# Hymba layer on one Trainium2 core: the seven-product up-projection in more chunks of both half-steps

## Chip, core and metric

The kernel runs on one core of one Trainium2 chip. The metric is the device time of one execution in microseconds (us). Before the change it is 1837.93 us, the median of three runs (1836.93 to 1838.51).

In the profile the engines are PE (TensorE, matmuls), PEld (its weight loads), DVE (VectorE), ACT (ScalarE), POOL (GpSimd) and SP (which issues the DMAs). L127 is line 127 of the kernel before.

## The reference, cut to what matters

One layer of a decoder, batch 1, 256 tokens, width 2048, everything in float32. A half-step is a gated feed-forward with inner width 5632; there are two of them, around a mixer of attention and a state-space part (S5).

```python
def rmsnorm(x, g):
    xf = x.astype(jnp.float32)
    y = xf * lax.rsqrt(jnp.mean(xf * xf, axis=-1, keepdims=True) + EPS)
    return (y * g.astype(jnp.float32)).astype(x.dtype)

def swiglu(x, w1, w3, w2):
    return (jax.nn.silu(x @ w1) * (x @ w3)) @ w2
...
        h = h + 0.5 * swiglu(rmsnorm(h, ffn1_norm[l]), ffn1_w1[l], ffn1_w3[l], ffn1_w2[l])
        proj = rmsnorm(h, mix_norm[l]) @ w_in[l]
...
        a = nsa_mixer(q, kc, vc, ksl, vsl, kw, vw, gates, rel_bias,
...
        s = s5_mixer(u_ssm, ssm_lam_re[l], ssm_lam_im[l], ssm_log_step[l], ssm_b_re[l], ssm_b_im[l],
...
        h = h + jnp.concatenate([a, s], axis=-1) @ w_out[l]
        h = h + 0.5 * swiglu(rmsnorm(h, ffn2_norm[l]), ffn2_w1[l], ffn2_w3[l], ffn2_w2[l])
    return rmsnorm(h, final_norm)
```

## The kernel before

**A product of float32.** PE multiplies float32r. Each operand is therefore split in a high part, a rounded copy made by ScalarE (L127), and a low part, the remainder, made by VectorE (L128), which needs the high part. A product is three matmuls: high x high, high x low, low x high. The activations are split once (`xh`, `xl`); the weights are split as they come: a DMA brings 256 rows x 512 columns (512 KB) into a tile `raw` (five buffers), and a pair of splits of 128x1024 makes `whi` and `wlo` (three buffers each). One such tile feeds 12 matmuls of 512 columns. Tiles called `wk` come from a pool of 48.

**A half-step** (`ffn`) goes through the inner width in 11 chunks of 512 columns. A chunk c has an up part (x @ w1 and x @ w3 over 16 blocks of the width, that is 8 pairs of blocks), the gates, 16 small transposes of the gates (L414) whose result is split again, and a down part (@ w2), which is done one chunk later: the order on PE is up(c), down(c-1) columns 0 and 1, transposes(c), down(c-1) columns 2 and 3. The results are added to `h` by VectorE (L357).

**Seven products.** In the second half-step the up part of every chunk runs through `up_wino`. For some pairs of blocks (`WINO`: 1, 3, 5) the 2x2 block product (two blocks of tokens x two blocks of the width, times w1 and w3 of two blocks) is done with seven block products in place of eight, after Winograd: 21 matmuls in place of 24. The price is sums. Of the weights: four sums of 128x512 (L318) and their splits, on VectorE and ScalarE, for each pair in each chunk; only w1 is split as a whole, of w3 one half. Of the activations ("left factor"): four sums per pair, made once, in `combine`, from the transposed activations while the output projection ends. The products are gathered in PSUM: `mm` (four banks: products 1, 5, 6, 7), `tp` (two banks: product 2 with the plain pairs' w1, product 3 with their w3, for the first tokens) and `sd` (two banks, the other tokens). `up_wino` thus uses all eight banks; the transposes use `tp` too. After the last pair of `WINO` VectorE gathers products 1, 5, 6 and 7 in four instructions (L336 to L339). Pairs not in `WINO` are "plain". In the first half-step all chunks are plain (L180 to L182).

**Side work.** Generators in `sides` get one step at each plain weight tile (`tick`). In the first half-step that is the preparation of S5 (`prepare`): it waits 40 tiles, then does a step at every second tile. A step is what stands between two `yield` in `s5_prepare`: 5 steps, then 28 for powers, 4 for products with B, 20 for matrices (with transposes and small matmuls on PE and copies out of PSUM, L598 and L612), and 24 for eight tables (L627, L628, L630), 81 in all. `up_wino` gives no step; the down parts of all chunks do.

**What sets the order.** A scheduler places all instructions on the engines' queues by priority as its own model of time sees them fit; each engine then runs its queue in that order, PE included. The splits of weights have a higher priority (`offset=50`). A buffer is taken when its former content has been read, so an instruction that fills a buffer waits for the readers.

Of the kernel before, what the change touches and what calls it, by code (L numbers as in the profile page):

```python
# [21 lines left out]
F32 = mybir.dt.float32  # L22
F32R = mybir.dt.float32r
# [18 lines left out]
WMAX = 536  # L42
WINO = (1, 3, 5)
WROW = 1152
# [27 lines left out]
def hymba_layer(tc, x, ffn1_norm, ffn1_w1, ffn1_w3, ffn1_w2, mix_norm, w_in,  # L72
# [22 lines left out]
    def work(shape, dtype=F32):  # L95
        return sp.tile(shape, dtype, name="wk", tag="wk")
# [106 lines left out]
    class Norm:  # L203
# [10 lines left out]

        def combine(self, pair, ps, scales):

            y, s = work([128, 2, T]), work([128, 4, 128])
            for k in range(2):
                S.activation(y[:, k, :], ps[:, k, :], AF.Identity, scale=scales[k])
            a11, a21, a12, a22 = (y[:, k, t * 128:t * 128 + 128] for k in range(2) for t in range(NT))  # L220
            V.tensor_tensor(s[:, 0, :], a21, a22, ALU.subtract)
            V.tensor_tensor(s[:, 2, :], a11, a21, ALU.subtract)
            V.tensor_tensor(s[:, 1, :], s[:, 0, :], a11, ALU.subtract)
            V.tensor_tensor(s[:, 3, :], a12, s[:, 1, :], ALU.add)
            sh, sl = work([128, 4, 128], F32R), work([128, 4, 128], F32R)
            split(sh, sl, s)
            self.wino[pair] = sh, sl

        def cols(self, n, wino=()):
            xh = xp.tile([128, 4, T], F32R, name="xh", tag="xh")  # L230
            xl = xp.tile([128, 4, T], F32R, name="xl", tag="xl")
            for kp in range(2):
                ps = tp_tile().rearrange("p (k t) -> p k t", k=2)
                for k in range(2):
                    kt = 4 * n + 2 * kp + k
                    for tt in range(NT):
                        PE.transpose(ps[:, k, tt * 128:tt * 128 + 128], h[:, tt, kt * 128:kt * 128 + 128], ident)
                for k in range(2):
                    g = self.gain * 16 + 4 * n + 2 * kp + k
                    split(xh[:, 2 * kp + k, :], xl[:, 2 * kp + k, :], ps[:, k, :], par[:, g:g + 1])  # L240
                if 2 * n + kp in wino:
                    g = self.gain * 16 + 4 * n + 2 * kp
                    self.combine(2 * n + kp, ps, [par[:, g + k:g + k + 1] for k in range(2)])
            self.x.append((xh, xl))
            self.square(n)
# [23 lines left out]

    def ffn(w1, w3, w2, xs, rstd, done, by_tokens=False, wino=()):  # L270
        last = FF // 512 - 1

        def up_wino(c):
# [25 lines left out]
            for p in range(KT // 2):  # L299
                raw1, raw3 = (wload(w[p * 256:p * 256 + 256, f], 512)[:, :, :512] for w in (w1, w3))  # L300
                end = p == KT // 2 - 1
                if p not in wino:
                    with tc.high_priority(offset=50):
# [5 lines left out]
                    continue  # L309
                done_ = p == max(wino)  # L310
                with tc.high_priority(offset=50):
# [77 lines left out]

        prev = None  # L390
        for c in range(FF // 512 + 1):
            if c < FF // 512 and wino:
                gates = up_wino(c)
# [275 lines left out]
    def prepare():  # L669
        for _ in range(40):  # L670
            yield
        for _ in s5_prepare():
            yield
            yield
        bias_prepare()
# [12 lines left out]
    prep = prepare()  # L688
    sides.append(prep)
    ffn(ffn1_w1[0], ffn1_w3[0], ffn1_w2[0], n1, n1.rstd(), nm.cols)  # L690
    drain(prep)
# [329 lines left out]
    for k0 in (8, 0):  # L1021
        if k0 == 0:
            drain(attn)
        for n in range(4):
# [4 lines left out]
            if k0 == 0:  # L1029
                n2.cols(n, WINO)  # L1030
    nf = Norm(0)
# [38 lines left out]

    ffn(ffn2_w1[0], ffn2_w3[0], ffn2_w2[0], n2, n2.rstd(), finish, by_tokens=True, wino=WINO)
    ctx.close()
# [23 lines left out]
```

## Time and profile before

| | us |
|---|---|
| median of 3 runs | 1837.93 |
| the profiled execution | 1839.61 |
| its span, first to last instruction | 1837.7 |
| PE busy | 1808.9 (98%) |
| PE weight loads | 1509.9 (82%) |
| VectorE busy | 1391.5 (76%) |
| ScalarE busy | 895.9 (49%) |

How to read it: matmuls overlap in the profile. A row's duration runs from its start to a modelled end, and the next one starts before that. How fast PE goes through its work is seen from start to start. The first half-step reaches to about 760 us, the second begins at about 1115 us; chunks take 64 to 70 us.

### The profile page before, as it was taken

The page shows a single profiled execution, that of the slowest core. Times are in us where ns is not written, and L with a number is a line of the kernel's source. Part 1 is how long each engine was busy: PE and PEld are TensorE (multiplying, and loading weights), DVE is VectorE, ACT ScalarE, POOL GpSimd, SP SyncE. Part 2 cuts the span into 40 slices and gives each one's busy share as a digit, 9 for nine tenths or more (in the row PEclk, how much of TensorE's full clock was granted, in tenths as well). Part 3 has the DMA queues.
Part 4 walks back from the last instruction along what each step waited for, and adds up shares of the span by engine and source line. Part 5 has one row for each costly group of instructions (what it writes and reads, how often), then busy time and mean ns, then how long its engine had stood idle before and what let it go on. Part 6 is the DMA issues. An engine that isn't in the chain of part 4 may idle for free. (4 is left out here: it accounts for less than half of the span.)

```text
span 1837.7 us, 24559 instructions
## 1 busy us (share of the span) xinstructions
PE 1808.9 (98%) x9266; PEld 1509.9 (82%) x9266; DVE 1391.5 (76%) x2003; ACT 895.9 (49%) x1233; POOL 14.7 (1%) x32
## 2 busy tenths in 40 slices
PE   8999999999999999999999999999999999999997
PEld 6888888888888888899988787788888888888886
DVE  5477666787987465789885668878887888789786
ACT  6434444433444444555537656545554554455454
POOL 0000000000000000000000000000000000000002
PEclk9999999999999999999999999999999999999999
DMA  7676666655566665555574366556666666666563
GB/s 240 188 214 188 193 186 193 185 174 180 179 194 190 194 191 188 171 152 152 147 220 143 111 187 187 194 182 199 192 206 185 204 206 194 194 195 204 179 205 135
DMA packets 193290, 340.88 MB, mean 185 GB/s; under 512 B 21034, under 2 KB 30868, under 8 KB 193172
## 3 DMA queue, kind: packets, MB, share of 16 engines
q1 hardware_dynamic: 193172, 339.31, 60.3%
q8 instruction: 73, 1.20, 0.3%
q14 instruction: 45, 0.37, 0.1%
HBM read 337.16 MB, written 2.11 MB: 185 GB/s over the span
## 5 line engine op out<-in xcount | busy, mean ns | idle before, releaser
L127 ACT ACTIVATE whi<-raw 128x1024 fp32r<-128x1024 f32 (+1 forms) x587 | 620.7, 1060 | 769.5 <-PE mm L182 499.9
L128 DVE SCALAR_TENSOR_TENSOR wlo<-raw,whi 128x1024 fp32r<-128x1024 f32 (+1 forms) x587 | 716.7, 1223 | 342.6 <-ACT whi L127 338.8
L180 PE MATMUL mm<-whi,xh 128*128 128x512 f32 x832 | 327.6, 394 | 2.0 <-ACT whi L127 2.0
L181 PE MATMUL mm<-wlo,xh 128*128 128x512 f32 x832 | 326.2, 392 | 0.0
L182 PE MATMUL mm<-whi,xl 128*128 128x512 f32 x832 | 325.7, 392 | 0.0
L180 PE MATMUL mm<-whi,wk 128*128 128x512 f32 x688 | 270.1, 393 | 0.0
L182 PE MATMUL mm<-whi,wk 128*128 128x512 f32 x688 | 268.2, 390 | 0.0
L181 PE MATMUL mm<-wlo,wk 128*128 128x512 f32 x688 | 268.0, 390 | 0.0
L180 PEld LDWEIGHTS mm<-whi,xh 128*128 128x128 f32 x832 | 156.6, 188 | 34.7 <-ACT whi L127 2.4
L181 PEld LDWEIGHTS mm<-wlo,xh 128*128 128x128 f32 x832 | 156.7, 188 | 33.0 <-DVE wlo L128 1.1
L182 PEld LDWEIGHTS mm<-whi,xl 128*128 128x128 f32 x832 | 156.6, 188 | 32.0 <-DVE xl L128 0.4
L182 PEld LDWEIGHTS mm<-whi,wk 128*128 128x128 f32 x688 | 129.1, 188 | 26.8
L180 PEld LDWEIGHTS mm<-whi,wk 128*128 128x128 f32 x688 | 129.2, 188 | 26.6 <-issue 0.6
L181 PEld LDWEIGHTS mm<-wlo,wk 128*128 128x128 f32 x688 | 129.3, 188 | 25.9
L357 DVE SCALAR_TENSOR_TENSOR h<-mm,h 128x512 f32<-128x512 f32 x176 | 114.3, 683 | 3.2 <-PE mm L369 2.5
L191 PE MATMUL mm<-xh,whi 128*128 128x256 f32 x384 | 112.7, 294 | 0.9 <-DVE wk L983 0.9
L127 ACT ACTIVATE wk<-wk 128x512 fp32r<-128x512 f32 x139 | 83.5, 626 | 55.5 <-DVE wk L318 49.7
L192 PE MATMUL mm<-xh,wlo 128*128 128x256 f32 x384 | 108.8, 283 | 0.0
L193 PE MATMUL mm<-xl,whi 128*128 128x256 f32 x384 | 108.8, 283 | 0.0
L284 PE MATMUL tp<-whi,xh 128*128 128x512 f32 x253 | 98.7, 391 | 2.2 <-DVE wk L128 1.1
L286 PE MATMUL tp<-wlo,xh 128*128 128x512 f32 x253 | 98.9, 392 | 1.2 <-DVE wlo L128 1.2
L287 PE MATMUL tp<-whi,xl 128*128 128x512 f32 x253 | 98.4, 390 | 0.0
(301 smaller groups left out, 2409.8 us busy)
## 6 DMA issues: line engine op xcount, KB each, us to landing
raw<-in_ffn_w_dram SPq DMA_DIRECT2D x528, 512.0 KB, 3.9
raw<-in_w_in_dram SPq DMA_DIRECT2D x48, 512.0 KB, 3.7
raw<-in_w_out_dram SPq DMA_DIRECT2D x32, 512.0 KB, 3.7
raw<-in_w_in_dram SPq DMA_DIRECT2D x8, 536.0 KB, 4.2
raw<-in_glu_w_dram SPq DMA_DIRECT2D x8, 512.0 KB, 4.6
h<-in_x_dram SPq DMA_DIRECT2D x4, 512.0 KB, 8.4
raw<-in_cmp_w_k_dram SPq DMA_DIRECT2D x4, 512.0 KB, 4.6
raw<-in_cmp_w_v_dram SPq DMA_DIRECT2D x4, 512.0 KB, 6.9
```

What stands on the lines that cost most here:

```text
L127: S.activation(hi, src, AF.Copy if isinstance(scale, float) else AF.Identity, scale=scale)
L128: V.scalar_tensor_tensor(lo, src, scale, hi.bitcast(F32), op0=ALU.mult, op1=ALU.subtract)
L180: PE.matmul(o, xh[:, t], hi[:, i, :n], start=kt == k0, stop=False)
L181: PE.matmul(o, xh[:, t], lo[:, i, :n], start=False, stop=False)
L182: PE.matmul(o, xl[:, t], hi[:, i, :n], start=False, stop=kt == k1 - 1)
L191: PE.matmul(o, wh, xh, start=kt == 0 and q % 2 == 0, stop=False, skip_group_check=True)
L192: PE.matmul(o, wl, xh, start=False, stop=False, skip_group_check=True)
L193: PE.matmul(o, wh, xl, start=False, stop=last, skip_group_check=True)
L284: PE.matmul(o, xh, wh, start=id(o) not in begun, stop=False)
L286: PE.matmul(o, xh, wl, start=False, stop=False)
L287: PE.matmul(o, xl, wh, start=False, stop=stop)
L357: V.scalar_tensor_tensor(o, p, 0.5, o, op0=ALU.mult, op1=ALU.add)
```

## The change

`WINO` becomes (0, 2, 4, 5): four pairs of eight. The seven-product form is used in chunks 1 to 5 of the first half-step and 1 to 10 of the second; chunk 0 of both is plain. The left factors are no longer made from the transposes' PSUM, but from the sum of `xh` and `xl`, as side work of chunk 0 (a step at each weight tile, the rest at the start of chunk 1). The S5 preparation starts in chunk 6 of the first half-step, without the wait of 40, and makes five steps in seven tiles.

```diff
-WINO = (1, 3, 5)
+WINO = (0, 2, 4, 5)
...
-        def combine(self, pair, ps, scales):
-
-            y, s = work([128, 2, T]), work([128, 4, 128])
-            for k in range(2):
-                S.activation(y[:, k, :], ps[:, k, :], AF.Identity, scale=scales[k])
-            a11, a21, a12, a22 = (y[:, k, t * 128:t * 128 + 128] for k in range(2) for t in range(NT))
...
-            sh, sl = work([128, 4, 128], F32R), work([128, 4, 128], F32R)
-            split(sh, sl, s)
-            self.wino[pair] = sh, sl
-
-        def cols(self, n, wino=()):
+        def combine(self):
+
+            for p in WINO:
+                xh, xl = (x[:, 2 * (p % 2):2 * (p % 2) + 2, :] for x in self.x[p // 2])
+                y, s = work([128, 2, T]), work([128, 4, 128])
+                V.tensor_tensor(y, xh.bitcast(F32), xl.bitcast(F32), ALU.add)
+                yield
+                a11, a21, a12, a22 = (y[:, k, t * 128:t * 128 + 128] for k in range(2) for t in range(NT))
+                V.tensor_tensor(s[:, 0, :], a21, a22, ALU.subtract)
+                V.tensor_tensor(s[:, 2, :], a11, a21, ALU.subtract)
+                V.tensor_tensor(s[:, 1, :], s[:, 0, :], a11, ALU.subtract)
+                V.tensor_tensor(s[:, 3, :], a12, s[:, 1, :], ALU.add)
+                yield
+                sh, sl = work([128, 4, 128], F32R), work([128, 4, 128], F32R)
+                split(sh, sl, s)
+                self.wino[p] = sh, sl
+                yield
+
+        def cols(self, n):
...
-                if 2 * n + kp in wino:
-                    g = self.gain * 16 + 4 * n + 2 * kp
-                    self.combine(2 * n + kp, ps, [par[:, g + k:g + k + 1] for k in range(2)])
...
-    def ffn(w1, w3, w2, xs, rstd, done, by_tokens=False, wino=()):
+    def ffn(w1, w3, w2, xs, rstd, done, by_tokens=False, wino=range(0), begin={}):
...
+        comb = xs.combine()
+        sides.append(comb)
         for c in range(FF // 512 + 1):
-            if c < FF // 512 and wino:
+            if c in begin:
+                sides.append(begin[c])
+            if c == wino[0]:
+                drain(comb)
+            if c in wino:
                 gates = up_wino(c)
...
     def prepare():
-        for _ in range(40):
+        for i, _ in enumerate(s5_prepare()):
             yield
-        for _ in s5_prepare():
-            yield
-            yield
+            if i % 5 < 2:
+                yield
         bias_prepare()
...
-    sides.append(prep)
-    ffn(ffn1_w1[0], ffn1_w3[0], ffn1_w2[0], n1, n1.rstd(), nm.cols)
+    ffn(ffn1_w1[0], ffn1_w3[0], ffn1_w2[0], n1, n1.rstd(), nm.cols, wino=range(1, 6), begin={6: prep})
...
-    ffn(ffn2_w1[0], ffn2_w3[0], ffn2_w2[0], n2, n2.rstd(), finish, by_tokens=True, wino=WINO)
+    ffn(ffn2_w1[0], ffn2_w3[0], ffn2_w2[0], n2, n2.rstd(), finish, by_tokens=True, wino=range(1, 11))
```

On PE's queue the program has 81 matmuls of 512 columns less. Lines of the kernel after are given by its own numbers: L321 is L318 of before, L287, L289 and L290 are L284, L286 and L287, L636, L637 and L639 are L627, L628 and L630.

VectorE, a steady chunk of the second half-step, around pair 5 (the last seven-product pair) and the plain pairs 6 and 7. Before, its remainder (wlo_12298), its four sums and their splits stand together, and the splits of pair 6 (wlo_12365, wlo_12369) and of pair 7 (wlo_12401) behind them:

```order
L128 SCALAR_TENSOR_TENSOR wlo_12298<-raw_12293,whi_12297 128x1024
L318 TENSOR_TENSOR wk_12305<-raw_12293,raw_12295 128x512
L318 TENSOR_TENSOR wk_12307<-wk_12305,raw_12295 128x512
L318 TENSOR_TENSOR wk_12309<-raw_12295 128x512
L318 TENSOR_TENSOR wk_12311<-wk_12307,raw_12293 128x512
L128 SCALAR_TENSOR_TENSOR wk_12314<-wk_12305,wk_12313 128x512
L128 SCALAR_TENSOR_TENSOR wk_12318<-wk_12307,wk_12317 128x512
L128 SCALAR_TENSOR_TENSOR wk_12322<-wk_12309,wk_12321 128x512
L128 SCALAR_TENSOR_TENSOR wk_12326<-wk_12311,wk_12325 128x512
L128 SCALAR_TENSOR_TENSOR wlo_12365<-raw_12360,whi_12364 128x1024
L128 SCALAR_TENSOR_TENSOR wlo_12369<-raw_12362,whi_12368 128x1024
L128 SCALAR_TENSOR_TENSOR wlo_12401<-raw_12396,whi_12400 128x1024
```

After (another chunk; pair 5 is wk_13445 to wk_13469, pair 6 wlo_13508 and wlo_13512, pair 7 wlo_13544):

```order
L128 SCALAR_TENSOR_TENSOR wlo_13508<-raw_13503,whi_13507 128x1024
L128 SCALAR_TENSOR_TENSOR wk_13445<-raw_13438,wk_13444 128x512
L321 TENSOR_TENSOR wk_13448<-raw_13436,raw_13438 128x512
L128 SCALAR_TENSOR_TENSOR wlo_13512<-raw_13505,whi_13511 128x1024
L321 TENSOR_TENSOR wk_13450<-wk_13448,raw_13438 128x512
L321 TENSOR_TENSOR wk_13452<-raw_13438 128x512
L321 TENSOR_TENSOR wk_13454<-wk_13450,raw_13436 128x512
L128 SCALAR_TENSOR_TENSOR wk_13457<-wk_13448,wk_13456 128x512
L128 SCALAR_TENSOR_TENSOR wlo_13544<-raw_13539,whi_13543 128x1024
L128 SCALAR_TENSOR_TENSOR wk_13461<-wk_13450,wk_13460 128x512
L128 SCALAR_TENSOR_TENSOR wk_13465<-wk_13452,wk_13464 128x512
L128 SCALAR_TENSOR_TENSOR wk_13469<-wk_13454,wk_13468 128x512
```

The wide splits of pairs 6 and 7 have moved in between the sums and the splits of pair 5. Two rows ahead of the first of these rows stands wlo_13441, the wide split of pair 5, whose `whi` buffer is that of pair 3's first tile; the buffer of whi_13543 is that of pair 5's own `whi`.

PE at the same place. Before, product 3 (tp_12068), 5 (mm_12064), 6 (mm_12065) and 7 (mm_12066) of pair 5 follow each other:

```order
L284 MATMUL tp_12068<-wk_12301,wk_9857 128x512
L286 MATMUL tp_12068<-wk_12302,wk_9857 128x512
L287 MATMUL tp_12068<-wk_12301,wk_9858 128x512
L284 MATMUL mm_12064<-wk_12313,wk_9857 128x512
L286 MATMUL mm_12064<-wk_12314,wk_9857 128x512
L287 MATMUL mm_12064<-wk_12313,wk_9858 128x512
L284 MATMUL mm_12065<-wk_12317,wk_9857 128x512
L286 MATMUL mm_12065<-wk_12318,wk_9857 128x512
```

After (product 5 is mm_13186, product 6 mm_13187; whi_13507, wlo_13508, whi_13511 and wlo_13512 are weights of pair 6):

```order
L287 MATMUL tp_13189<-whi_13507,xh_10459 128x512
L287 MATMUL mm_13186<-wk_13456,wk_10777 128x512
L289 MATMUL tp_13189<-wlo_13508,xh_10459 128x512
L290 MATMUL tp_13189<-whi_13507,xl_10460 128x512
L289 MATMUL mm_13186<-wk_13457,wk_10777 128x512
L290 MATMUL mm_13186<-wk_13456,wk_10778 128x512
L287 MATMUL tp_13190<-whi_13511,xh_10459 128x512
L287 MATMUL mm_13187<-wk_13460,wk_10777 128x512
L289 MATMUL tp_13190<-wlo_13512,xh_10459 128x512
L290 MATMUL tp_13190<-whi_13511,xl_10460 128x512
L287 MATMUL sd_13192<-whi_13511,xh_10459 128x512
L289 MATMUL sd_13192<-wlo_13512,xh_10459 128x512
```

Matmuls of pair 6 now stand between those of pair 5. The 13 seven-product chunks that follow another one look the same; the first of each half-step has a mixed order of its own.

VectorE in the up part of a chunk of the first half-step in which S5's tables are made. Before (chunk 7):

```order
L627 TENSOR_TENSOR wk_4060<-wk_1339,wk_2044 128x512
L128 SCALAR_TENSOR_TENSOR wlo_4131<-raw_4128,whi_4130 128x1024
L628 TENSOR_TENSOR wk_4107<-wk_1340,wk_2043 128x512
L627 TENSOR_TENSOR wk_4183<-wk_1339,wk_2043 128x512
L128 SCALAR_TENSOR_TENSOR wlo_4150<-raw_4147,whi_4149 128x1024
L630 TENSOR_TENSOR wk_4060<-wk_4060,wk_4107 128x512
L628 TENSOR_TENSOR wk_4185<-wk_1340,wk_2044 128x512
L627 TENSOR_TENSOR wk_4184<-wk_1339,wk_2044 128x512
L128 SCALAR_TENSOR_TENSOR wlo_4168<-raw_4165,whi_4167 128x1024
```

After (chunk 9):

```order
L636 TENSOR_TENSOR wk_5605<-wk_3737,wk_4271 128x512
L637 TENSOR_TENSOR wk_5607<-wk_3738,wk_4272 128x512
L636 TENSOR_TENSOR wk_5606<-wk_3737,wk_4272 128x512
L639 TENSOR_TENSOR wk_5605<-wk_5605,wk_5607 128x512
L128 SCALAR_TENSOR_TENSOR wlo_5635<-raw_5632,whi_5634 128x1024
L637 TENSOR_TENSOR wk_5629<-wk_3738,wk_4271 128x512
L636 TENSOR_TENSOR wk_5669<-wk_3737,wk_4271 128x512
L128 SCALAR_TENSOR_TENSOR wlo_5654<-raw_5651,whi_5653 128x1024
L639 TENSOR_TENSOR wk_5606<-wk_5606,wk_5629 128x512
L637 TENSOR_TENSOR wk_5671<-wk_3738,wk_4272 128x512
L636 TENSOR_TENSOR wk_5670<-wk_3737,wk_4272 128x512
L128 SCALAR_TENSOR_TENSOR wlo_5677<-raw_5674,whi_5676 128x1024
```

Between one weight split and the next there were one to three instructions of the tables, and after a few tiles none; now up to four stand ahead of a split, and the runs with three are longer.

## Rows read from the trace of the kernel before

**Rows 1.** The page: span, busy time of three engines, the chain by engine
```profile
span 1837.7 us, 24559 instructions
PE 1808.9 (98%) x9266; PEld 1509.9 (82%) x9266; DVE 1391.5 (76%) x2003; ACT 895.9 (49%) x1233; POOL 14.7 (1%) x32
PE 37%; DVE 1%; DMA 1%; ACT 0%; issue 0%; ACTq 0%; DVEq 0%
```

**Rows 2.** Busy time by stretch; columns: us, busy us (instructions) per engine, clock, DMA
```profile
core 0: us, PE busy (x) PEld busy (x) DVE busy (x) ACT busy (x) POOL busy (x), PEclk, DMA share, GB/s
...
622.40:687.70 65.30, 65.30 (x294) 54.13 (x293) 36.09 (x36) 27.46 (x28) 0.00 (x0) 1.00 0.62 191
...
1447.00:1510.00 63.00, 63.00 (x283) 52.25 (x283) 53.41 (x68) 32.27 (x41) 0.00 (x0) 1.00 0.65 197
...
1110.00:1235.00 125.00, 120.44 (x521) 93.52 (x520) 106.52 (x156) 68.00 (x99) 0.00 (x0) 1.00 0.60 190
1250.00:1375.00 125.00, 125.00 (x562) 103.66 (x561) 105.94 (x135) 64.80 (x81) 0.00 (x0) 1.00 0.64 198
```

**Rows 3.** Timeline, PE, seven-product chunk: start us, duration us, instruction
```profile
1499.62 0.39 PE L287 MATMUL sd<-whi,xl 128*128 128x512 f32 x1
...
1509.82 0.39 PE L287 MATMUL sd<-whi,xl 128*128 128x512 f32 x1
```

**Rows 4.** Groups, 1447 to 1510: xcount | busy us, mean ns | idle before
```profile
L128 DVE SCALAR_TENSOR_TENSOR wlo<-raw,whi 128x1024 fp32r<-128x1024 f32 x21 | 25.6, 1222 | 8.0 <-ACT whi L127 7.8
L128 DVE SCALAR_TENSOR_TENSOR wk<-wk 128x512 fp32r<-128x512 f32 x12 | 7.6, 683 | 0.0
...
L318 DVE TENSOR_TENSOR wk<-wk,raw 128x512 f32<-128x512 f32 x6 | 4.1, 689 | 0.1
...
L127 ACT ACTIVATE whi<-raw 128x1024 fp32r<-128x1024 f32 x21 | 22.1, 1058 | 23.1 <-PE sd L287 11.8 <-PE mm L182 8.9 <-issue 1.5
L127 ACT ACTIVATE wk<-wk 128x512 fp32r<-128x512 f32 x12 | 7.2, 627 | 4.9 <-DVE wk L318 4.8
```

**Rows 5.** Timeline around pair 5 of one chunk; in brackets idle time and releaser
```profile
1380.11 2.49 DVE L128 SCALAR_TENSOR_TENSOR wk<-wk 128x512 fp32r<-128x512 f32 x4
1383.12 2.58 DVE L128 SCALAR_TENSOR_TENSOR wlo<-raw,whi 128x1024 fp32r<-128x1024 f32 x2 [0.52 <-ACT whi L127]
...
1391.98 0.39 PE L284 MATMUL tp<-whi,xh 128*128 128x512 f32 x1
...
1392.18 1.06 ACT L127 ACTIVATE whi<-raw 128x1024 fp32r<-128x1024 f32 x1 [6.29 <-PE sd L287]
...
1393.27 2.59 DVE L128 SCALAR_TENSOR_TENSOR wlo<-raw,whi 128x1024 fp32r<-128x1024 f32 x2 [3.54 <-ACT whi L127]
```

**Rows 6.** Timeline, first half-step, S5's tables between weight splits
```profile
531.22 1.24 DVE L128 SCALAR_TENSOR_TENSOR wlo<-raw,whi 128x1024 fp32r<-128x1024 f32 x1
532.35 0.71 DVE L630 TENSOR_TENSOR wk<-wk 128x512 f32<-128x512 f32 x1
532.95 1.14 DVE L628 TENSOR_TENSOR wk<-wk 128x512 f32<-128x512 f32 x1
533.98 1.15 DVE L627 TENSOR_TENSOR wk<-wk 128x512 f32<-128x512 f32 x1
535.02 1.25 DVE L128 SCALAR_TENSOR_TENSOR wlo<-raw,whi 128x1024 fp32r<-128x1024 f32 x1
...
541.17 1.26 DVE L128 SCALAR_TENSOR_TENSOR wlo<-raw,whi 128x1024 fp32r<-128x1024 f32 x1
...
542.48 0.19 PEld L181 LDWEIGHTS mm<-wlo,xh 128*128 128x128 f32 x1 [0.38 <-DVE wlo L128]
```

**Rows 7.** Timeline, second half-step, behind the transposes of chunk 0
```profile
1164.05 0.87 PE L414 MATMUL tp<-cst,wk 128*128 128x128 f32 x6
...
1165.27 1.29 DVE L128 SCALAR_TENSOR_TENSOR wk<-tp,wk 128x512 fp32r<-128x512 f32 x2 [1.27 <-ACT wk L127]
...
1166.01 0.50 PE L284 MATMUL tp<-whi,xh 128*128 128x512 f32 x1 [1.08 <-DVE wk L128]
```

More of the change, by code (lines that the diff above doesn't have):

```diff
@@ L213, in square @@
                 S.activation(junk, h[:, tt, n * 512:(n + 1) * 512], AF.Square, accum_out=self.ssq[:, tt, n:n + 1])
-        def combine(self, pair, ps, scales):
-            y, s = work([128, 2, T]), work([128, 4, 128])
-            for k in range(2):
-                S.activation(y[:, k, :], ps[:, k, :], AF.Identity, scale=scales[k])
-            a11, a21, a12, a22 = (y[:, k, t * 128:t * 128 + 128] for k in range(2) for t in range(NT))
[L221 to L224, printed above, removed]
-            sh, sl = work([128, 4, 128], F32R), work([128, 4, 128], F32R)
-            split(sh, sl, s)
-            self.wino[pair] = sh, sl
-        def cols(self, n, wino=()):
+        def combine(self):
[15 more added lines that the diff above has]
+        def cols(self, n):
             xh = xp.tile([128, 4, T], F32R, name="xh", tag="xh")
@@ L301, in up_wino @@
                 end = p == KT // 2 - 1
-                if p not in wino:
+                if p not in WINO:
                     with tc.high_priority(offset=50):
@@ L309, in up_wino @@
                     continue
-                done_ = p == max(wino)
+                done_ = p == max(WINO)
                 with tc.high_priority(offset=50):
@@ L1029, in hymba_layer @@
             if k0 == 0:
-                n2.cols(n, WINO)
+                n2.cols(n)
     nf = Norm(0)
```

## The prediction

> **What bounds the kernel now.** I read the page first: TensorE is busy 98% of the span, VectorE 76%, ScalarE 49%, and the chain that ended last consists of PE nearly alone [rows 1]. Then the stretches: in plain chunks of the first half-step and in seven-product chunks of the second, PE is busy in all of its time, VectorE in 36 and 53 us of 65.3 and 63 [rows 2]. Then the matmuls themselves: from 1499.62 to 1509.82 there are 45 steps from start to start, so a 512-column matmul costs **0.2267 us**, not the 0.39 that its row shows as duration [rows 3]. The granted clock there is 1.00, the level of 2.4 GHz [rows 2]. So inside the half-steps a matmul less is 0.2267 us less, as long as weights are ready. Where that fails is visible too: of two stretches of 125 us, the entry of the second half-step holds 521 matmuls and a later one 562 [rows 2]; with 24 and 16 small transposes taken out it is 497 against 546, 49 x 0.2267 = 11.1 us, less about 0.9 for the eight extra transposes: **10.2 us are lost at that entry**.
>
> **What is removed on PE.** A pair costs 24 matmuls plain and 21 in seven products. Before: 11 chunks x 3 pairs = 33 pairs. After: 5 x 4 in the first half-step and 10 x 4 in the second = 60. The order has 81 matmuls less. 81 x 0.2267 = **-18.4 us**, if PE stays fed.
> The Trainium skill (TensorE: Matmul & The Clock Gate, Back-to-back issue gap) gives 131 ns per matmul at 512 columns in a sustained stream; by it the sum would be -10.6 us. The trace disagrees with that figure: 0.2267 us over 45 steps [rows 3].
>
> **What that costs on VectorE and ScalarE.** A plain pair takes two splits of 128x1024; a seven-product pair takes one of them, five of 128x512 and four sums. By the rows, 1.22, 0.68 and 0.69 us each; in a queue without gaps the next one starts after 1.14, 0.60 and 0.63 [rows 4, 5]. So a fourth pair adds -1.14 + 3.0 + 2.5 = 4.4 us of VectorE per chunk: 53.4 of 63 becomes about 57.8 of 62.3. ScalarE gains -1.06 + 5 x 0.63 = 2.1 us on 32 of 63 [rows 2, 4]: hidden. The mean fits, so the order inside a chunk decides. Three weight buffers exist, so each wide split waits until PE has finished the tile three before it: PE's next matmul starts at 1391.98, ScalarE at 1392.18, its 1.06 us end, VectorE starts at 1393.27 [rows 5]. Bytes are the same, in 1% less time.
>
> *The tightest place, pairs 4 and 5 in a row.* Call R the moment at which PE is done with the first weight tile of pair 3. From R, ScalarE needs 0.20 + 1.06, VectorE starts at R + 1.30. In its new order nine instructions then end in the remainder of pair 5's first sum: three wide splits, two narrow ones and four sums (the last row wk_13457): 3 x 1.14 + 2 x 0.60 + 4 x 0.61 = 7.06, and 0.68 for itself: R + 9.04, seen by PE about 0.06 later. In PE's new order this is the 41st matmul after R: R + 40 x 0.2267 = R + 9.07. So it is late by 0.03 us. The next, wk_13461, comes after a wide split for pair 7 and ends at R + 10.8; PE wants it at R + 49 x 0.2267 = R + 11.1. PE's order has nine matmuls of pair 6 moved between those of pair 5, and only they make this fit. I put down **0.2 us** per chunk for the 13 steady ones, +2.6; the bounds are 0 and 1.0. Before, VectorE stood idle 3.54 us at this place [rows 5], so it had cover that is used up now.
>
> *Two entries.* In each first seven-product chunk no down-projection separates the transposes of the gates from product 2, which wants the same PSUM banks. The trace shows this once: transposes until 1164.9, the remainder of the split until 1166.0, PE idle 1.08 [rows 7]. It now happens in the first half-step as well: **+2.0 us** (1 to 3). In the second half-step the first chunk is plain, with no left factors to wait for. Of the 10.2 us I leave this 2.0 and 1.7 for small waits behind the output projection: **-6.5 us** (-4 to -8.5).
>
> *Left factors.* They were made in the output projection with two scaled copies on ScalarE; now each is one sum of 128x512, four of 128x128, one split: some 2 us of VectorE, eight times. They lie in the two chunks 0, where VectorE is busy 36 us of 65 [rows 2]: nothing, and if that cover were gone, 8 us per half-step.
>
> **S5 preparation, closer together.** 81 steps at 1.4 weight tiles each instead of 2: 113 of the 120 tiles of chunks 6 to 10, with all their DMAs and small matmuls. No queue is added, and its consumers come later. What matters is its tables. L627 and L628 take 1.11 to 1.17 us and L630 0.70; the next starts after 1.03 and 0.60 [rows 6]. One weight tile gives PE 12 x 0.2267 = 2.72 us. When a split comes together with L630, L628 and L627, it is 3.80 us from split to split (531.22 to 535.02) [rows 6]. A split is ready 2 x 2.72 + 0.23 - 0.20 - 1.06 - 0.03 - 1.22 = 3.16 us before PE wants it; behind the transposes of the gates 4.06.
> Before, the densest run is 5.43 + 2.34 + 3.80 + 2.34 + 3.80 + 2.78 = 20.49 against 6 x 2.72 = 16.32: 4.17 against a lead of 4.06. And the trace shows that the lead was gone: at 542.48 PE waited for the split that ended at 542.43 [rows 6]. So this reckoning holds.
> After: in the up part of chunk 9 the order gives 5.07 + 3.20 + 3.80 + 3.80 + 2.78 + 3.80 = 22.45, 6.13 over, less 3.15: 3.0 us late. Then, from chunk 9's transposes on, the same run as before with two more of 3.80: 28.09 - 21.76 = 6.33, less 4.06: 2.3 us. Together **+5.3 us**. Bounds 2 (small matmuls of the preparation give VectorE time) and 8 (each late tile restarts PE 0.11 us slower; steps of the k0 part wait for VectorE in PE's queue).
>
> **Sum.** -18.4 - 6.5 + 2.0 + 2.6 + 5.3 = -15.0. Against the profiled execution, 1839.6: 1824.6. That one lies 1.7 above the median of 1837.9; so **1823**.
>
> **Rivals.**
> A, *the fill does not hold, and it is slower.* If VectorE reaches pair 5 late, PE has used up its matmuls of pair 6, and the wide split for pair 7, which itself waits for PE's product 2 of pair 5, stands ahead of three narrow ones that pair 5 needs. From there it is 0.20 + 1.06 + 0.04 + 1.14 + 0.68 + 0.06 = 3.18 us against 1.59 of PE work: 1.6 us in each of 15 chunks, +24 instead of +2.6: 1844. Gain turns to loss from 17.6 / 15 = 1.2 us per chunk. For it: VectorE has 12 instructions back to back here and 0.03 us to lack; 93% load. Against it: these durations vary by 1% [rows 4], and both ends of the reckoning hang on the same moment R. A lateness of 0.6 to 1.1 us per chunk (9 to 16.5 in place of 2.6) is more likely than the whole: 1829 to 1837.
> The Trainium skill (Perfetto Trace Analysis, Identifying the Most-Contended Engine) would rate VectorE by busy share and TensorE by its weight loads: 82% for the loads [rows 1] and, by my estimate of 147 us more work, 84% for VectorE, so VectorE would be the engine that limits. That speaks for A. In this trace PE is gapless at 53 of 63 us of VectorE [rows 2]; no row shows it at 93%.
> B, *the tables cost nothing* and the entry gives all that it can: -18.4 - 8.5 + 1 = -26: 1812 to 1817. For it: the scheduler might have placed tables where slack is. Against it: the order shows four of 3.80 in a run.
> That the change does not do what it says is excluded: the order holds the 81 matmuls less.
>
> **How the numbers follow.** Forecast (1817 to 1830) 0.64. B 0.10. The weak form of A (1830 to 1841) 0.17, of which 0.08 is still faster. Full A 0.09. A measurement of this kernel tells about 0.2% from no change, that is 1834.3 and 1841.6. Faster 0.64 + 0.10 + 0.08 = 0.82, same 0.09, slower 0.09. The range of 1815 to 1837 takes in the forecast, half of B and most of the weak A.
>
> **What would show it.** PE at 0.2267 us per matmul everywhere; 62.3 to 62.9 us of work in a window that held 63. In the steady chunks waits of PE for narrow VectorE splits (wk) of at most 0.2 us, one or two per chunk, in pair 5: over 0.5 proves A. In chunks 9 and 10 of the first half-step waits for wlo in two groups of some 3 and 2.3 us. One wait of 1 to 1.5 us behind the transposes of each chunk 0. The entry of the second half-step with some 545 matmuls in 125 us in place of 521. Wrong it would be if VectorE starts pair 5's sums later than R + 4.8, or if waits appear in the mixer, whose order on PE is the same.

## The result and the profile after

The changed kernel takes **1826.3 us** (median; 1825.3 to 1827.6) beside 1838.2 for the kernel before on the same chip: a ratio of 0.9936, 95% interval 0.9919 to 0.9954. It was run once more with the later experiments: 1824.8 beside 1837.8, ratio 0.9930 (0.9914 to 0.9947). So it is faster by 12 to 13 us; 15 were forecast, and the time lies in the range. The profiled execution has a span of 1824.2 us beside 1837.7.

The page of the changed kernel, with the lines that answer to [rows 1]:

```profile
span 1824.2 us, 24780 instructions
PE 1793.3 (98%) x9185; PEld 1491.7 (82%) x9185; DVE 1527.3 (84%) x2284; ACT 937.6 (51%) x1344; POOL 14.8 (1%) x32
PE 51%; DVE 3%; issue 1%; DMA 1%; ACT 0%; SPq 0%; ACTq 0%; DVEq 0%
```

PE has 81 instructions less and is still busy in 98% of the span. VectorE went from 76 to 84%, and 3% of the chain of work is now VectorE's, where it was 1%: there are places at which PE waits for it.

Busy time by stretch in the changed kernel, for [rows 2]: a seven-product chunk of the first half-step, one of the second, the entry of the second half-step, and a later stretch of the same 125 us.

```profile
core 0: us, PE busy (x) PEld busy (x) DVE busy (x) ACT busy (x) POOL busy (x), PEclk, DMA share, GB/s
311.60:376.90 65.30, 65.30 (x293) 53.73 (x292) 57.91 (x77) 34.82 (x45) 0.25 (x2) 1.00 0.65 198
1399.00:1462.00 63.00, 63.00 (x279) 51.69 (x277) 56.97 (x76) 33.82 (x45) 0.00 (x0) 1.00 0.65 198
1110.00:1235.00 125.00, 123.87 (x549) 100.52 (x548) 108.26 (x165) 68.06 (x90) 0.00 (x0) 1.00 0.67 201
1300.00:1425.00 125.00, 125.00 (x558) 102.80 (x558) 113.07 (x150) 67.51 (x89) 0.00 (x0) 1.00 0.65 198
```

The entry holds 549 matmuls where [rows 2] had 521, and its PE is idle for 1.1 us in place of 4.6.

The timeline around pair 5 in one steady chunk (start us, duration us, instruction; in brackets the idle time before it and who ended it), for [rows 5]:

```profile
1365.38 0.39 PE L287 MATMUL tp<-whi,xh 128*128 128x512 f32 x1
...
1366.72 1.23 DVE L128 SCALAR_TENSOR_TENSOR wlo<-raw,whi 128x1024 fp32r<-128x1024 f32 x1 [0.56 <-ACT whi L127]
...
1373.75 0.68 DVE L128 SCALAR_TENSOR_TENSOR wk<-wk 128x512 fp32r<-128x512 f32 x1
...
1374.48 0.19 PEld L289 LDWEIGHTS mm<-wk 128*128 128x128 f32 x1 [0.30 <-DVE wk L128]
1374.49 0.50 PE L289 MATMUL mm<-wk 128*128 128x512 f32 x1
1374.82 0.39 PE L290 MATMUL mm<-wk 128*128 128x512 f32 x1
```

With R = 1365.4 VectorE starts at R + 1.3, the narrow split ends at 1374.43 = R + 9.0, and PE takes it at R + 9.1. That is the reckoning of the prediction. Forty steps from R would have had PE there at 1374.45; it starts 0.04 us later, and then the first matmul after the wait needs 0.33 us to the next one in place of 0.2267. All 13 steady chunks show the same to 0.01 us: the narrow split ends at R + 9.05.

Behind the transposes of each chunk 0 stands one wait. The second half-step, for [rows 7] (the first half-step has the same at 61.63, 1.12 us):

```profile
1152.85 0.87 PE L423 MATMUL tp<-cst,wk 128*128 128x128 f32 x6
1154.12 1.28 DVE L128 SCALAR_TENSOR_TENSOR wk<-tp,wk 128x512 fp32r<-128x512 f32 x2
1154.86 0.50 PE L287 MATMUL tp<-whi,xh 128*128 128x512 f32 x1 [1.13 <-DVE wk L128]
```

In chunk 9 of the first half-step VectorE's tables stand between the weight splits, for [rows 6]:

```profile
624.44 1.25 DVE L128 SCALAR_TENSOR_TENSOR wlo<-raw,whi 128x1024 fp32r<-128x1024 f32 x1
625.57 0.72 DVE L639 TENSOR_TENSOR wk<-wk 128x512 f32<-128x512 f32 x1
626.17 1.15 DVE L637 TENSOR_TENSOR wk<-wk 128x512 f32<-128x512 f32 x1
627.19 1.15 DVE L636 TENSOR_TENSOR wk<-wk 128x512 f32<-128x512 f32 x1
628.22 1.26 DVE L128 SCALAR_TENSOR_TENSOR wlo<-raw,whi 128x1024 fp32r<-128x1024 f32 x1
...
629.53 0.50 PE L181 MATMUL mm<-wlo,xh 128*128 128x512 f32 x1 [0.73 <-DVE wlo L128]
```

From split to split it is 3.78 us, for 2.72 us of PE's work. The waits of PE from 600 to 690 us (who waits for whom, us in all, times, longest):

```profile
PE mm L181 <- DVE wlo L128: 3.2, 5, 0.8
```

Counted from start to start, with the 0.11 us that each restart takes, these waits are 4.7 us: 2.5 from 625 to 636, 2.2 from 667 to 677.

### The profile page after: what moved, and what is told of

Its sections match the earlier page's. It is cut to its first block, busy times and chain, and to the rows that moved or that the text cites. A ratio compares the mean times of both kernels' runs of the same rounds, so it can differ in the third digit from the quotient of the medians.

```text
span 1824.2 us, 24780 instructions
## 1 busy us (share of the span) xinstructions
PE 1793.3 (98%) x9185; PEld 1491.7 (82%) x9185; DVE 1527.3 (84%) x2284; ACT 937.6 (51%) x1344; POOL 14.8 (1%) x32
## 4 chain that ended last, share of the span: by engine, by line
PE 51%; DVE 3%; issue 1%; DMA 1%; ACT 0%; SPq 0%; ACTq 0%; DVEq 0%
PE mm L180 7%; PE mm L181 7%; PE mm L182 7%; PE tp L287 3%; PE tp L290 3%; PE tp L289 3%; PE sd L287 2%; PE sd L289 2%; PE sd L290 2%; PE mm L289 2%; PE mm L287 2%; PE mm L290 2%; PE mm L191 1%; PE mm L192 1%; PE mm L193 1%
## 5 line engine op out<-in xcount | busy, mean ns | idle before, releaser
L127 ACT ACTIVATE whi<-raw 128x1024 fp32r<-128x1024 f32 (+1 forms) x560 | 593.3, 1059 | 689.3 <-PE mm L182 368.7
L128 DVE SCALAR_TENSOR_TENSOR wlo<-raw,whi 128x1024 fp32r<-128x1024 f32 (+1 forms) x560 | 684.2, 1223 | 204.9 <-ACT whi L127 202.3
L181 PE MATMUL mm<-wlo,wk 128*128 128x512 f32 x688 | 268.4, 390 | 0.8 <-DVE wlo L128 0.8
L180 PE MATMUL mm<-whi,xh 128*128 128x512 f32 x576 | 227.9, 396 | 2.0 <-ACT whi L127 2.0
L181 PE MATMUL mm<-wlo,xh 128*128 128x512 f32 x576 | 226.9, 394 | 2.5 <-DVE wlo L128 2.5
L182 PE MATMUL mm<-whi,xl 128*128 128x512 f32 x576 | 225.8, 392 | 0.0
L127 ACT ACTIVATE wk<-wk 128x512 fp32r<-128x512 f32 x252 | 151.0, 622 | 121.5 <-DVE wk L321 113.1
L128 DVE SCALAR_TENSOR_TENSOR wk<-wk 128x512 fp32r<-128x512 f32 x252 | 166.2, 685 | 2.1 <-ACT wk L127 2.1
L181 PEld LDWEIGHTS mm<-wlo,wk 128*128 128x128 f32 x688 | 129.3, 188 | 27.0 <-DVE wlo L128 1.2
L181 PEld LDWEIGHTS mm<-wlo,xh 128*128 128x128 f32 x576 | 108.5, 188 | 26.4 <-DVE wlo L128 4.8
L180 PEld LDWEIGHTS mm<-whi,xh 128*128 128x128 f32 x576 | 108.4, 188 | 24.8 <-ACT whi L127 2.4
L182 PEld LDWEIGHTS mm<-whi,xl 128*128 128x128 f32 x576 | 108.3, 188 | 22.1 <-DVE xl L128 0.4
L287 PE MATMUL tp<-whi,xh 128*128 128x512 f32 x300 | 117.1, 390 | 2.2 <-DVE wk L128 2.2
L289 PE MATMUL tp<-wlo,xh 128*128 128x512 f32 x300 | 116.9, 390 | 0.0
L290 PE MATMUL tp<-whi,xl 128*128 128x512 f32 x300 | 116.8, 389 | 0.0
```

The lines of the kernel that those rows point to most:

```text
L127: S.activation(hi, src, AF.Copy if isinstance(scale, float) else AF.Identity, scale=scale)
L128: V.scalar_tensor_tensor(lo, src, scale, hi.bitcast(F32), op0=ALU.mult, op1=ALU.subtract)
L180: PE.matmul(o, xh[:, t], hi[:, i, :n], start=kt == k0, stop=False)
L181: PE.matmul(o, xh[:, t], lo[:, i, :n], start=False, stop=False)
L182: PE.matmul(o, xl[:, t], hi[:, i, :n], start=False, stop=kt == k1 - 1)
L287: PE.matmul(o, xh, wh, start=id(o) not in begun, stop=False)
```

## The experiments

All times are medians. Where a figure is said to be of the changed kernel, its profiled execution above is meant.

**1. Pairs apart.** In `up_wino` pair 6 takes the place of pair 5:

```
-WINO = (0, 2, 4, 5)
+WINO = (0, 2, 4, 6)
```

> The changed kernel with seven-product pairs 0, 2, 4, 6 in place of 0, 2, 4, 5: as many matmuls, as much VectorE work (84% of the span), but no two seven-product pairs in a row. Theory (VectorE's lead is used up by two such pairs in a row): the wait of PE behind pair 5's narrow split goes, and with it the 0.33 us by which a steady chunk (63.78) is longer than before's 64.13 less three matmuls of 0.2267; 13 steady chunks give back some 4.3 us: about 1822, a chunk of 63.45. Rival (the mean load of VectorE, or something that comes with any fourth pair, lengthens the chunk): chunks stay at 63.8 and the time at 1826.

It takes 1823.0 us (ratio to before 0.9924, 0.9908 to 0.9941). The first matmul of a down part begins one chunk, so two such starts give the length of a chunk; this kernel, then the changed one:

```profile
1333.29 0.47 PE L180 MATMUL mm<-whi,wk 128*128 128x512 f32 x1
...
1396.89 0.47 PE L180 MATMUL mm<-whi,wk 128*128 128x512 f32 x1
```

```profile
1335.26 0.48 PE L180 MATMUL mm<-whi,wk 128*128 128x512 f32 x1
...
1398.99 0.48 PE L180 MATMUL mm<-whi,wk 128*128 128x512 f32 x1
```

That is 63.60 and 63.73 us; over the nine steady chunks of the second half-step the mean is 63.61 and 63.79. The kernel before has 64.13:

```profile
1410.46 0.48 PE L180 MATMUL mm<-whi,wk 128*128 128x512 f32 x1
...
1474.59 0.48 PE L180 MATMUL mm<-whi,wk 128*128 128x512 f32 x1
```

Three matmuls less than that is 63.45 us, a chunk with no further wait. The wait behind pair 5's narrow split is gone, as the theory said. But only 0.18 of the 0.34 us went with it. The rest is in both kernels. Here it is in this one, at the first sum of pair 0:

```profile
1411.00 1.28 DVE L360 SCALAR_TENSOR_TENSOR h<-mm,h 128x512 f32<-128x512 f32 x2
1411.73 0.19 PEld L287 LDWEIGHTS mm<-wk 128*128 128x128 f32 x1 [0.24 <-DVE h L360]
1411.75 0.48 PE L287 MATMUL mm<-wk 128*128 128x512 f32 x1
```

The first product of pair 0 with a sum wants a bank of `mm` that the down part before it has filled, and VectorE has only just added that to `h`: 0.09 us per chunk. With pairs 1, 3, 5 (experiment 7) no such step stands in the chunk, which takes 64.17 us. So the wait comes with pair 0 or with a fourth pair; the row speaks for pair 0, but no run has four pairs without it.

**2. Three pairs in a row.**

```
-WINO = (0, 2, 4, 5)
+WINO = (0, 3, 4, 5)
```

> The changed kernel with seven-product pairs 0, 3, 4, 5: same count of matmuls and same mean load of VectorE, but three seven-product pairs in a row. Theory (lead): such a pair takes 1.14 + 5 x 0.60 + 4 x 0.63 = 6.7 us of VectorE against 21 x 0.2267 = 4.76 us of PE, so each takes 1.9 us of lead; two in a row end 0.04 us late, so a third in a row makes PE late by some 1.9 us per chunk, 15 times: +28, about 1854 (1841 to 1864 for 1.0 to 2.5 us per chunk). Rival (mean load): no change, 1826. PE then waits for narrow splits (wk) in pairs 4 and 5.

It takes 1828.7 us (0.9953, 0.9938 to 0.9968), 2 to 4 us more than the changed kernel and not 28. The steady chunk is 63.88 us. The theory has the right place and a wrong size. The timeline of pairs 3 and 5 in one chunk of this kernel shows why:

```profile
1357.43 1.28 DVE L128 SCALAR_TENSOR_TENSOR wk<-wk 128x512 fp32r<-128x512 f32 x2
...
1366.63 0.39 PE L289 MATMUL mm<-wk 128*128 128x512 f32 x1
...
1367.31 0.39 PE L289 MATMUL mm<-wk 128*128 128x512 f32 x1
...
1377.68 2.49 DVE L128 SCALAR_TENSOR_TENSOR wk<-wk 128x512 fp32r<-128x512 f32 x4
...
1379.04 0.48 PE L289 MATMUL mm<-wk 128*128 128x512 f32 x1
```

Two narrow splits of pair 3 end at 1358.1 and 1358.7, 8.5 us before PE takes them (two further ones follow singly); those of pair 5 come 0.1 to 0.4 us ahead. With one plain pair ahead, in the changed kernel, most of those of pair 4 are 4.1 us ahead. I had taken the lead for one and the same before every row. It isn't: only the wide splits are held by the three buffers. Narrow ones go to the pool of 48, and in two plain pairs VectorE makes them far ahead. The third pair then uses up what the second plain pair had laid by. This is read from the timelines; no run changes the number of buffers.

**3. Tables spaced.**

```
-            if i % 5 < 2:
+            if i >= 57 or i % 4 == 0:
                 yield
```

> The changed kernel in which the last 24 steps of the S5 preparation, its tables, come at 2 weight tiles each as before (the other 57 steps at 1.25); everything else as in the changed kernel. Theory: the 4.6 us of waits for wlo in chunks 9 and 10 of the first half-step come from tables too close together on VectorE. By the order of VectorE the densest run is now 22.3 against 16.3 us with a lead of 4.06 behind the transposes, late by 0.1, and the other by nothing: about 4.5 us less, 1822. Rival (the waits come from something else in these chunks, transfers or the small matmuls): 1826, with the waits where they were.

It takes 1821.2 us (0.9914, 0.9899 to 0.9928), 4 to 5 us less than the changed kernel; 4.5 were forecast. From 600 to 690 us no wait of PE is left in the view that showed 3.2 us; the group of L181 over the same stretch says it for PE and its weight loads together. The changed kernel, then this one:

```profile
  DVE wlo L128: 9.3, 13
```

```profile
  DVE wlo L128: 0.5, 2
```

So the waits came from the tables' density on VectorE. The other steps of the preparation come closer together here (1.25 tiles each), and no wait of PE came of that.

**4. Five pairs.**

```
-WINO = (0, 2, 4, 5)
+WINO = (0, 2, 3, 5, 6)
```

> The changed kernel with five seven-product pairs, 0, 2, 3, 5, 6: 45 matmuls fewer, 45 x 0.2267 = -10.2 us if PE stays fed, which would be 1816. Theory (lead): VectorE has 4.4 us more in each of 15 chunks, 62.2 of 62.7 us, and two couples in a row with one plain pair between them, which returns 5.44 - 2.28 = 3.2 of the 3.9 us of lead that a couple takes; the second couple is late by some 0.7 us, and VectorE, full, no longer catches up: 1 to 2 us per chunk, +15 to +30: 1821 to 1836, most likely 1830, and no gain over four pairs. Rival (mean load alone decides and 99% still fits): 1816.

It takes 1847.6 us (1.0058, 1.0043 to 1.0073): slower than the kernel before, with 126 matmuls less than it. The theory had no gain either, but 1830 (1821 to 1836). One steady chunk by stretch, this kernel and then the changed one:

```profile
1413.71:1478.38 64.67, 64.26 (x284) 51.49 (x283) 62.09 (x85) 36.09 (x50) 0.00 (x0) 1.00 0.63 195
```

```profile
1335.26:1398.99 63.73, 63.73 (x287) 52.47 (x285) 57.80 (x77) 34.28 (x46) 0.00 (x0) 1.00 0.64 199
```

A chunk should be 63.45 - 3 x 0.2267 = 62.77 us and is 64.67: 1.9 are lost, the upper end of what was expected. VectorE is busy 62.1 of 64.7 us, 96%, and idle for 2.6; 2.1 of these are six waits of wide splits for ScalarE's high parts. The longest waits of PE's weight loads in that chunk, narrow splits first:

```profile
PEld sd L289 <- DVE wk L128: 0.9, 2, 0.7
PEld mm L289 <- DVE wk L128: 0.7, 2, 0.5
PEld mm L287 <- ACT wk L127: 0.5, 2, 0.3
```

What I had not reckoned is the first seven-product chunk of each half-step, in which no down part lies ahead: 57.8 and 57.1 us in place of 53.0 and 52.9, with fewer matmuls. The 13 steady chunks, from transposes to transposes, take 64.8 in the mean for 63.8, 12.6 us in all; with these 4.7 and 4.2 that is 21.5, for 21.3 between the medians.

**5 and 6. The two halves of the change, each alone.** First only the first half-step, with the output projection (left factors in `cols` as before) and the second half-step of before:

```
-                n2.cols(n)
+                n2.cols(n, (1, 3, 5))
...
-    ffn(ffn2_w1[0], ffn2_w3[0], ffn2_w2[0], n2, n2.rstd(), finish, by_tokens=True, wino=range(1, 11))
+    ffn(ffn2_w1[0], ffn2_w3[0], ffn2_w2[0], n2, n2.rstd(), finish, by_tokens=True, wino=range(0, 11), pairs=(1, 3, 5))
```

> The part of the change in the first half-step alone (seven products in its chunks 1 to 5, left factors in its chunk 0, preparation in its chunks 6 to 10); the second half-step and the output projection as before. In the changed kernel's trace everything up to the mixer is 5.7 us shorter than before. Theory (the parts add up: -13.6 for 60 matmuls, +1.6 entry, +1.6 steady chunks, +4.6 tables): 1838 - 5.7 = about 1832. Rival (the small part of the gain has to do with what comes behind, the mixer or the second half-step): 1828 or 1836.

1833.8 us (0.9974, 0.9965 to 0.9984). Then only the second half-step, with the preparation paced as before:

```
-    ffn(ffn1_w1[0], ffn1_w3[0], ffn1_w2[0], n1, n1.rstd(), nm.cols, wino=range(1, 6), begin={6: prep})
+    ffn(ffn1_w1[0], ffn1_w3[0], ffn1_w2[0], n1, n1.rstd(), nm.cols, begin={0: prep})
```

> The part of the change in the second half-step alone (pairs 0, 2, 4, 5 in chunks 1 to 10, chunk 0 plain, left factors made there); the first half-step and the preparation as before. Theory: -4.8 for 21 matmuls, -7.0 at the entry, +3.0 for the steady chunks: -8.8, about 1829, and together with the first half alone the whole -13 to -14.5. Rival (entry gains only because of something in the first half-step): 1834.

1830.0 us (0.9957, 0.994 to 0.9973). Against 1838.4 that is -4.6 and -8.4, in sum -13.0; the whole gives -12 to -13. The parts add up.

**7. Three pairs, chunk 0 plain.** The second half alone, with the pairs of before:

```
-WINO = (0, 2, 4, 5)
+WINO = (1, 3, 5)
```

> As the second half alone, but with pairs 1, 3, 5 as before in chunks 1 to 10: only chunk 0 has become plain and the left factors are made there. Nine matmuls more than before, 9 x 0.2267 = +2.0. Theory (the 10 us lost at the entry come from left factors and their cover in chunk 0): the entry gives 7.0, in all -5.0: about 1833, steady chunks at 64.13. Rival (they come from the output projection and stay): 1840.

1832.6 us (0.9968, 0.9956 to 0.9979). The entry of the second half-step in this kernel:

```profile
1110.00:1235.00 125.00, 125.00 (x562) 102.75 (x562) 101.59 (x149) 66.61 (x87) 0.00 (x0) 1.00 0.66 202
```

PE is busy in all of it, with 562 matmuls, as many as later. So most of the loss of 10 us came with left factors made in the output projection and seven products in the first chunk, not from the output projection as such. This run changes both at once and doesn't separate them. From the last matmul of 256 columns in the mixer to the last of all, this kernel takes 802.6 us and the one before 809.6: 7.0 less, with 2.0 us more of matmuls, hence 9.1 at the entry. In the changed kernel that stretch takes 800.7: 8.9 less, of which 4.8 are matmuls, and 3.1 were given to nine steady chunks: 7.2 at the entry. Most of the difference is the wait behind the transposes. Here it doesn't exist: the first pair is plain, and its matmuls into `sd` run while VectorE empties the bank of `tp`.

**8. Pairs apart and tables spaced**, both edits of 1 and 3.

> The changed kernel with pairs 0, 2, 4, 6 and with the tables at 2 weight tiles per step: both single edits together. They lie in different chunks, so theory: they add up, 1826.3 - 3.3 - 5.1 = 1818 (1816 to 1820). Rival (the gain of one was partly chance of the runs, 1 to 2 us): 1820 to 1822.

1818.8 us (0.9894, 0.9879 to 0.9908), for 1818 expected. They add up, as far as medians from different chips can tell.

**9. The changed kernel again.**

> The changed kernel as it is, beside the two that follow on one chip. Expected 1826.3 again. Its mixer tells whether the 1.5 us by which mixers of the kernels so far differ, with the same order on PE, goes with the program or with the single execution.

1824.8 us; span 1822.3, 1.9 less than in its first profile. Laid side by side, matmul by matmul, the two executions run within 0.3 us of each other up to 935 us; between 935 and 949, in the mixer, the first one loses 1.7 us, and from there on they keep that distance to 0.2. In the first one PE waits there for a DMA:

```profile
949.14 0.38 PE L840 MATMUL tp<-wk 128*128 128x30 f32 x2 [1.81 <-DMA wk<-in_cmp_w_k_dram]
```

This transfer of 64 KB was issued at 943.8 us in both; it landed after 5.2 us in the first and after 3.5 in the second, where PE didn't wait for it. In the kernel before it landed after 3.6 us. So this scatter is the time of one transfer and goes with the single execution, not with the program.

**10. Half of the tables' products on GpSimd.** The kernel of experiment 1 with

```
-            V.tensor_tensor(t.rearrange("p j (m n) -> p j m n", m=8), f[1], g[q], ALU.mult)
+            G.tensor_tensor(t.rearrange("p j (m n) -> p j m n", m=8), f[1], g[q], ALU.mult)
```

> The changed kernel with pairs 0, 2, 4, 6 and one of the two products of each table made on GpSimd in place of VectorE; tables at 1.4 weight tiles as in the changed kernel. Theory (waits for wlo come from VectorE's load in these runs of tables): 16 x 1.03 us leave VectorE there, by its order the densest run is below its lead, the 4.6 us of waits go: 1823.0 - 4.6 = 1818.4. Rival (GpSimd is slow at it and VectorE's sum, which needs both products, waits with the weight split behind it): no row of the kernel before shows such an instruction on GpSimd; if it takes over 2.7 us the waits grow: 1823 to 1835.

1828.6 us (0.9949, 0.9934 to 0.9963): 5.6 more than the same kernel with all on VectorE, 5.2 if each is taken from the kernel before on its own chip. The waits from 570 to 690 us are

```profile
PE mm L181 <- DVE wlo L128: 5.4, 5, 2.1
PE tp L605 <- DVE wk L600: 2.5, 1, 2.5
```

and two instances of the product in the timeline of GpSimd and VectorE show what happens:

```profile
607.45 1.41 POOL L637 TENSOR_TENSOR wk<-wk 128x512 f32<-128x512 f32 x1 [14.55 <-DVE wk L600]
...
626.83 2.15 POOL L637 TENSOR_TENSOR wk<-wk 128x512 f32<-128x512 f32 x1 [4.35 <-DVE wk L639]
627.70 2.37 DVE L128 SCALAR_TENSOR_TENSOR wlo<-raw,whi 128x1024 fp32r<-128x1024 f32 x1
```

The shortest of these products takes 1.41 us; most, beside VectorE, 2.0 to 3.5. And the weight split beside it takes 2.37 in place of 1.22 us. It ends at 630.07; the product of GpSimd had ended at 628.98, and 628.98 + 1.1 = 630.07. It looks as if the split had stood until the other was done. The other order occurs too: at 633.5 two splits take their usual 1.21 us each, and the product that began beside them takes 3.48. Both engines lose, and the split is what PE waits for.

The Trainium skill (SBUF — State Buffer, SBUF: two separate sides) says that the two engines share a pair of ports: when a VectorE instruction has two inputs in SBUF and the GpSimd one reads SBUF, whichever starts first holds the pair for its whole instruction while the other stands. These durations agree with that; no run here separates it from another cause.

**11. One chunk more, with GpSimd.** Pairs 0, 2, 4, 6; seven products in chunks 1 to 6, preparation in 7 to 10, tables as in 10.

```
-            if i % 5 < 2:
+            if i >= 66:
...
-    ffn(ffn1_w1[0], ffn1_w3[0], ffn1_w2[0], n1, n1.rstd(), nm.cols, wino=range(1, 6), begin={6: prep})
+    ffn(ffn1_w1[0], ffn1_w3[0], ffn1_w2[0], n1, n1.rstd(), nm.cols, wino=range(1, 7), begin={7: prep})
```

> Pairs 0, 2, 4, 6, seven products in chunks 1 to 6 of the first half-step instead of 1 to 5, preparation in chunks 7 to 10 (first 66 steps at 1 weight tile, the last 15 at 2), one of two products of each table on GpSimd. Against spread and spaced (1818.8): 12 matmuls less and one more restart, -2.5; tables denser again, late by about 1 us in chunk 9 by the order of VectorE: 1817.3 (1816 to 1819). Rival (GpSimd slow, or the preparation's small matmuls, 1 step per tile, make PE wait): 1820 or more.

1825.5 us (0.9933, 0.9918 to 0.9948). The rival came: GpSimd's products took 1.93 us on average, and PE waits 8.6 us from 570 to 690, 4.8 of them for weight splits and 3.8 in the preparation's small matmuls.

**12. One chunk more, tables on VectorE.** Pairs 0, 2, 4, 6; the preparation starts in the down part of chunk 6, 57 steps at one weight tile, the tables at two.

```
-            if i % 5 < 2:
+            if i >= 57:
...
-    ffn(ffn1_w1[0], ffn1_w3[0], ffn1_w2[0], n1, n1.rstd(), nm.cols, wino=range(1, 6), begin={6: prep})
+    ffn(ffn1_w1[0], ffn1_w3[0], ffn1_w2[0], n1, n1.rstd(), nm.cols, wino=range(1, 7), begin={6: prep})
```

> Pairs 0, 2, 4, 6, seven products in chunks 1 to 6 of the first half-step, preparation from chunk 6 on (first 57 steps at 1 weight tile, tables at 2), all tables on VectorE. Against spread and spaced (1818.8): 12 matmuls less, 12 x 0.2267 = -2.7, one more restart and PSUM wait, +0.15; the tables stand as in spread and spaced: 1816.3 (1815 to 1818). Rival (the preparation's small matmuls at 1 step per tile wait for VectorE in PE's queue, or its first steps fall into the full seven-product chunk 6): 1819 or more.

**1815.4 us** (0.9878, 0.9862 to 0.9895), the best version. From 570 to 690 us the view of waits has no line for PE. The page:

```profile
span 1813.2 us, 24808 instructions
PE 1786.5 (99%) x9173; PEld 1491.7 (82%) x9173; DVE 1548.6 (85%) x2324; ACT 946.2 (52%) x1361; POOL 14.8 (1%) x32
```

## Why the prediction was right, point by point

The terms of the sum, forecast and as read in the changed kernel's trace:

| term | forecast us | measured us | from |
|---|---|---|---|
| 81 matmuls less | -18.4 | -18.4 | 9266 and 9185 instructions on PE, 0.2267 us apart |
| entry of the second half-step | -6.5 | -7.2 | stretch behind the mixer (7) |
| wait in the first half-step's entry | +2.0 | +1.6 | 1.3 + 0.11 + 0.24 behind the transposes |
| steady chunks | +2.6 | +4.7 | 13 chunks, 63.81 us in the mean for 63.45 |
| tables | +5.3 | +4.7 | restarts included; 4 to 5 by (3) |
| sum | -15.0 | -14.6 | |

The step that was mis-sized is the one on the steady chunks. That the sums agree to 0.4 us is in part luck: the steady chunks cost 2.1 more than forecast, and the three other terms that were estimates 1.7 less. The spans differ by 13.5 us; what is missing to 14.6 is 1.0 in the mixer, where the late transfer of (9) falls. The second profile of the changed kernel, with a span of 1822.3, has 15.4. The medians differ by 12 to 13: I moved the profiled gain onto the median as it stood, and a single execution isn't known to better than 1 to 2 us.

*Pairs 4 and 5.* The reckoning from R held to 0.1 us. The term was still too small, 0.36 in place of 0.2 per chunk. Two things were missing: a wait of 0.04 us costs 0.15, since the matmul after it needs 0.11 more; and the wait of 0.09 at pair 0 for the bank of the down part. Experiment 1 shows both: the first goes, the second stays. The last 0.1 is in no single row.

*Rival A, the fill doesn't hold.* It did not come: pair 5's first narrow split came before the wide one and 0.04 us late, and no steady chunk lost more than 0.7 us. Experiment 4 shows a state like the one that A describes: with VectorE at 96% of a chunk, PE waits at several places in each, and 45 matmuls less cost 21 us.

The Trainium skill (Perfetto Trace Analysis, Identifying the Most-Contended Engine) would have had VectorE, at 84%, limit the changed kernel against 82% of weight loads. The trace doesn't agree: in the chunk of experiment 1 VectorE is busy 57.9 of 63.60 us (91%) and the weight loads 52.6 (83%), and the chunk is only 0.15 us longer than the 63.45 of PE's own work. What was lost had to do with order, not with the share.

*Tables and rival B.* They came as worked out, in two groups of 2.5 and 2.2 us (3.0 and 2.3 forecast), and experiment 3 removed them. Rival B, tables that cost nothing, would have needed the spacing of that experiment.

*Entries.* In the second half-step 549 matmuls for a forecast of 545, and one wait behind the transposes in each. The price of that wait was named, its remedy not: a plain first pair (7). A chunk has eight of these transposes, in the kernel as in the trace; the 16 in the description of the kernel is wrong, and the prediction counted with eight.

*The two signs of being wrong.* Both came, narrowly read, and neither meant what it was meant to. VectorE starts pair 5's sums at R + 4.82 in the steady chunks, past the R + 4.8 that was to show an error; the reckoning itself gives 4.78, so the mark stood only 0.02 us beyond what was expected. And a wait did appear in the mixer, 1.8 us in one of two executions of the same program: the transfer of (9).

## What to carry to other kernels

Work out a queue's lead at its densest place, from a common moment and in the queue's own order; the mean load says little (84% of VectorE cost 0.34 us a chunk or 0.16, by where the pairs stood). Ask of each buffer class separately how far ahead it lets the engine run: here, as the timelines read, three buffers held the wide splits and 48 did not hold the narrow ones, and a forecast that took one lead for both had +28 us where 2 to 4 came. Side work beside a tight queue is spaced by its cost, not by its count of steps, and moving half of its products to GpSimd, beside which VectorE ran longer, cost 5 us.

## What was not expected of the hardware

**GpSimd and VectorE took longer side by side**: 1.41 us became up to 3.5 on one, 1.22 became 2.37 on the other (10).

**The clock can fall in the middle of a kernel.** With five pairs, in the second half-step's first seven-product chunk, PE waited for ScalarE and VectorE, and from 1198.8 to 1202.8 only five matmuls began. In that stretch the granted clock went from 1.00 to 0.50, which is from 2.4 to 1.2 GHz, and behind it five matmuls in a row came 0.427 us apart in place of 0.227, until it rose again at about 1205. One of the waits, and the stretches:

```profile
1200.88 1.09 PE L287 MATMUL mm<-wk 128*128 128x512 f32 x2 [1.67 <-ACT wk L127]
```

```profile
1200.00:1202.00 2.00, 1.07 (x2) 0.37 (x2) 1.72 (x3) 2.00 (x5) 0.00 (x0) 0.92 0.75 270
1202.00:1204.00 2.00, 1.78 (x4) 1.49 (x5) 1.97 (x4) 0.86 (x2) 0.00 (x0) 0.50 0.88 264
1204.00:1206.00 2.00, 2.00 (x8) 1.54 (x7) 1.07 (x2) 0.00 (x0) 0.00 (x0) 0.72 1.02 364
1206.00:1208.00 2.00, 2.00 (x11) 1.65 (x10) 2.00 (x4) 0.48 (x1) 0.00 (x0) 1.00 0.29 110
```

Five matmuls, 0.2 us more each: 1.0 us that no wait in the profile shows. The first half-step's first seven-product chunk has the same: PE waited 1.7 us for ScalarE, and from 104 to 106 us the granted clock is 0.50. In the changed kernel, whose longest wait in either chunk is 1.1 us, the clock stays at 1.00 in both.
